# S5 states by real scans in turning frames, and the LRU convolution read from the banks one tile ahead

## The chip, the cores and the metric

The kernel runs on one core of a Trainium2 chip. The metric is device time in microseconds (us) for one execution; the median of three runs is given. TensorE (PE) multiplies matrices, VectorE (DVE) and GpSimd (POOL) work elementwise, ScalarE (ACT) applies functions, SyncE (SP) issues most of the transfers. Each engine works through its own queue in order; engines wait for each other on semaphores. Operands lie in SBUF; TensorE writes into banks of PSUM.

## The reference

One layer of a backbone: a modulated norm, one input projection `w_in`, three token mixers (RG-LRU, RWKV-7, S5), gates `zg`, an output projection and a feed-forward block. 256 context and 1024 latent tokens, width 1024, each branch 512 wide. What the change touches:

```python
# RG-LRU, both directions, on xc = conv of 4 taps of xa
a = jnp.exp(log_a)                     # log_a = -8 * gate_r * softplus(-lam)
u = jnp.sqrt(-jnp.expm1(2.0 * log_a)) * (gate_i * xc)
h = linear_scan(a, u, h0, reverse)     # h[t] = a[t] h[t-1] + u[t]
y = jax.nn.gelu(ga) * (hs[0] + hs[1])

# S5, 32 groups of 16 channels and 64 complex states, both directions
bu = einsum(u, bb)                     # complex
h[t] = lb * h[t-1] + bu[t]             # lb = mag * exp(i * ang), constant in t
y = einsum(h_re, c_re) - einsum(h_im, c_im)
```

The S5 scan runs over latent tokens in column-major order after the context; eight tokens make one step of the kernel's state, so there are 160 states (32 of the context, 128 of the latents) for each of 32 groups, with the multiplier lb to the eighth power.

## The kernel before

Activations lie with channels on the partitions and 1280 tokens in a row. Every product with `w_in` is made of three float32r products of split operands (`xh`, `xl` with `wh`, `wl`): `inproj` for the branches (L1302), the generator `zg` for the 24 column tiles of the gates (L1308). A column tile of zg has two halves of 24 matmuls 128x512; its weights come by DMA, `zh` is a copy by ScalarE (L1294), `zl` a subtraction by VectorE (L1295), and the result leaves through a tanh (L1344). zg is the filler: `s.fill(n)` issues n units of three such matmuls between the steps of other stages. How many is set by the constants at L1103 (FF in the S5 front, FL behind an LRU tile, FB in the S5 back end). What is left when the RWKV chain begins is issued at once. 1152 matmuls of zg exist in all.

`run` writes the stages in this order: front (norm, modulation, S5 inputs) with `s5_setup`; `mod2`, a matrix-vector product with `w_mod` on VectorE (L1257 to L1283) that is drawn on by `mix` and `side` between other steps; four times `s5_front`; `s5_scan`; four `lru_tile`; eight `s5_carry`; eight `s5_back`; S5 output, RWKV low-rank inputs, four RWKV pairs, chain, merge, feed-forward. A scheduler of the framework decides from this program the fixed order of each engine's queue; work of neighbouring stages is mixed in it.

`s5_front(q)` (L410 to L477) forms the input matrices of eight groups on VectorE (L418 to L423, L434, L436) and GpSimd (L435), transposes them on TensorE (L442), and multiplies (L467): 160 columns for a group, 128 matmuls in all. ScalarE and VectorE copy the banks into `s5_h` (L474 to L477), one half of the partitions forward, the other backward.

`s5_scan` (L489 to L508) is the recurrence on GpSimd: 31 steps over five blocks of 32 states at once, four operations of 128x320 each (L498 to L501), then three steps that carry the blocks' ends. `s5_carry` (L510 to L523) adds the carried states into the blocks after the LRU, mostly on VectorE, a part on GpSimd. `s5_back` (L534 to L567) forms the outputs.

`lru_tile(j)` (L118 to L182) takes one of four tiles of 128 channels: inproj, ScalarE copies the banks to `xap` (L132), VectorE makes the four taps of the convolution from there (L137, L140), then for each direction six gate matmuls (L150), sigmoid and tanh on ScalarE (L153, L155), Exp and Tanh (L159, L160), three elementwise operations and the square root (L161 to L165), the scan on VectorE (L168, L171, L173). At the end GpSimd adds the directions (L176), ScalarE takes the gelu of a further inproj (L180), GpSimd multiplies (L181). `xap` and the second direction's `gi` share one buffer, so the next tile's copies wait for L176.

Of the kernel before, what the change touches and what calls it, by code (L numbers as in the profile page):

```python
# [93 lines left out]
class LruMixin:  # L94
    def lru_setup(s, pool):
# [22 lines left out]
    def lru_tile(s, j, pool):  # L118
        nc = s.nc
        bd = pool.tile([P, 2, 2, P], F32, name="lru_bd", tag="lru_bd")  # L120
# [13 lines left out]
        cw, cb = s.pv("conv_w"), s.pv("conv_b")
        for o, t0, n in ((0, 0, NCTX), (259, NCTX, NLAT)):
            x = xc[:, t0 : t0 + n]
            nc.vector.tensor_scalar(x, xap[:, o : o + n], cw[:, j : j + 1], cb[:, j : j + 1],  # L137
                                    op0=ALU.mult, op1=ALU.add)
            for k in range(1, 4):
                nc.vector.scalar_tensor_tensor(x, xap[:, o + k : o + k + n], cw[:, 4 * k + j : 4 * k + j + 1], x,  # L140
                                               op0=ALU.mult, op1=ALU.add)
        hs = []
        for d in range(2):
            gr = pool.tile([P, NT], F32, name="gr", tag="gr")
            gi = pool.tile([P, 1286], F32, name="gi", tag="xap")[:, 0:NT] if d else \
                pool.tile([P, NT], F32, name="gi", tag="gi")
            for w, g in enumerate((gr, gi)):
                for t0, n in ((0, NCTX), (NCTX, 512), (NCTX + 512, 512)):
                    ps = s.aux()
                    nc.tensor.matmul(ps[:, :n], bd[:, w, d, :], xc[:, t0 : t0 + n], start=True, stop=True)  # L150
                    q = slice(4 * d + j, 4 * d + j + 1)
                    if w:
                        nc.scalar.activation(g[:, t0 : t0 + n], ps[:, :n], AF.Tanh, scale=0.5, bias=s.lru_hb[:, q])  # L153
                    else:
                        nc.scalar.activation(g[:, t0 : t0 + n], ps[:, :n], AF.Sigmoid, bias=s.pv("ba")[:, q])  # L155
            c8 = s.lru_c8[:, 4 * d + j : 4 * d + j + 1]
            a = pool.tile([P, NT], F32, name="a", tag="a")
            th = pool.tile([P, NT], F32, name="th", tag="th")
            nc.scalar.activation(a, gr, AF.Exp, scale=c8)  # L159
            nc.scalar.activation(th, gr, AF.Tanh, scale=c8)  # L160
            nc.vector.scalar_tensor_tensor(gi, gi, 1.0, xc, op0=ALU.add, op1=ALU.mult)  # L161
# [1 line left out]
            nc.vector.scalar_tensor_tensor(th, gr, 1.0, th, op0=ALU.add, op1=ALU.mult)
            nc.scalar.activation(th, th, AF.Sqrt, scale=-0.25)
            nc.vector.tensor_tensor(gi, gi, th, op=ALU.mult)  # L165
            h = gi
            if d == 0:
                nc.vector.tensor_tensor_scan(h, a, gi, 0.0, ALU.mult, ALU.add)  # L168
            else:
                c, l = slice(0, NCTX), slice(NCTX, NT)  # L170
                nc.vector.tensor_tensor_scan(h[:, c][:, ::-1], a[:, c][:, ::-1], gi[:, c][:, ::-1], 0.0,  # L171
                                             ALU.mult, ALU.add)
                nc.vector.tensor_tensor_scan(h[:, l][:, ::-1], a[:, l][:, ::-1], gi[:, l][:, ::-1], h[:, 0:1],  # L173
                                             ALU.mult, ALU.add)
            hs.append(h)
# [26 lines left out]
class S5Mixin:  # L202
    def s5_setup(s, pool, fpool, tpool):
# [140 lines left out]
        cr, ci = T(32, 32, keep=pool), T(32, 32, keep=pool)
        V.tensor_copy(cr[:, 0], pr[:, 8])
        V.tensor_copy(ci[:, 0], pi[:, 8])
        for n_ in (1, 2, 4, 8, 16):
            cmul(cr, ci, n_, n_, 0, n_ - 1)
        s.s5_cp = (cr, ci)
# [1697 lines left out]
```

## Time and profile before

| | us |
|---|---|
| median of three runs (2294.9 to 2298.51) | 2295.26 |
| the profiled execution | 2292.87 |
| its span, first to last instruction | 2291.1 |
| mean granted TensorE clock | 0.951 |
| busy: TensorE / VectorE / GpSimd / ScalarE | 2071.9 / 1623.8 / 1135.8 / 925.9 |

The profiled execution's own time is the span and 1.8 us around it. Busy time of matmuls is modelled, with starts closer than their lengths because they are pipelined; the distance of two starts tells the price. A clock of 1.0 is TensorE's full speed. The 40 slices of the page's second part show TensorE at eight to nine tenths over most of the span and GpSimd near full from the fifth to the tenth slice.

### The profile page before, as it was taken

To read this page: it belongs to the slowest core of one execution; us is meant where nothing else is said; L and a number is where in the kernel's file an instruction comes from. 1 tells how busy PE (TensorE), PEld (TensorE's weight loads), DVE (VectorE), ACT (ScalarE), POOL (GpSimd) and SP (SyncE) were. 2 spreads that over 40 slices of the span, in tenths; PEclk is the share of its full clock that TensorE was granted. 3 is DMA by queue.
4 is the path that set the end of the run, shared out by engine and by line. 5 is a ranking of instruction groups with operands and counts; after the bars stand their busy time and mean duration, and the time that the engine had idled before them with its cause. 6 is when DMAs were issued, how large, how long until landed. Compare 5 with 4: busy or idle time off the path is not lost. (4 is left out here: it accounts for less than half of the span.)

```text
span 2291.1 us, 38462 instructions
## 1 busy us (share of the span) xinstructions
PE 2071.9 (90%) x14441; PEld 1650.5 (72%) x14441; DVE 1623.8 (71%) x2253; ACT 925.9 (40%) x1740; POOL 1135.8 (50%) x1260
## 2 busy tenths in 40 slices
PE   5989978887899988898599999889799999999998
PEld 3868856565778777786467676668588888887786
DVE  5656698889665787889963346853985666568977
ACT  5314345433343646453533433424533232324453
POOL 3662389954522483948100023343564545437656
PEclk7989989998999999999699999999899999999999
DMA  6634322321662635354877768554132323238334
GB/s 258 169 113 114 96 62 76 96 81 60 138 179 75 188 104 156 98 144 122 240 194 165 181 164 210 158 196 152 61 125 92 115 88 120 97 115 298 113 117 153
DMA packets 371751, 314.08 MB, mean 137 GB/s; under 512 B 67239, under 2 KB 313198, under 8 KB 370542
## 3 DMA queue, kind: packets, MB, share of 16 engines
q1 hardware_dynamic: 369134, 304.28, 45.8%
q10 hardware_dynamic: 1728, 6.29, 0.8%
q8 instruction: 114, 1.87, 0.3%
q0 software_dynamic: 704, 1.05, 0.2%
q14 instruction: 71, 0.58, 0.1%
HBM read 217.20 MB, written 94.35 MB: 136 GB/s over the span
## 5 line engine op out<-in xcount | busy, mean ns | idle before, releaser
L1562 PE MATMUL mm<-q,wt 128*128 128x512 f32 x1584 | 376.5, 398 | 4.8 <-DVE q L1476 3.8
L1562 PEld LDWEIGHTS mm<-q,wt 128*128 128x128 f32 x1584 | 299.5, 189 | 77.6 <-DVE q L1476 4.2
L1302 PE MATMUL mm<-xh,wh 128*128 128x512 f32 (+1 forms) x576 | 215.8, 382 | 8.3 <-ACT ya L180 4.8
L1786 PE MATMUL mm<-wt,hk 128*128 128x512 f32 x924 | 218.3, 398 | 5.0 <-DVE hk L1476 4.1
L1302 PE MATMUL mm<-xl,wh 128*128 128x512 f32 (+1 forms) x576 | 215.9, 382 | 1.2 <-DVE xl L1218 1.2
L1786 PEld LDWEIGHTS mm<-wt,hk 128*128 128x128 f32 x924 | 174.5, 189 | 48.7 <-DVE hk L1476 5.5
L1308 PE MATMUL mm<-xh,zh 128*128 128x512 f32 x384 | 161.9, 422 | 9.9 <-ACT zge L1344 5.8
L1308 PE MATMUL mm<-xl,zh 128*128 128x512 f32 x384 | 160.9, 419 | 0.0
L1302 PE MATMUL mm<-xh,wl 128*128 128x512 f32 (+1 forms) x576 | 140.3, 381 | 6.9 <-DVE wl L1295 6.4
L1302 PEld LDWEIGHTS mm<-xh,wh 128*128 128x128 f32 x576 | 115.1, 200 | 28.7 <-ACT ya L180 5.7
L1302 PEld LDWEIGHTS mm<-xl,wh 128*128 128x128 f32 x576 | 114.8, 199 | 19.5 <-DVE xl L1218 1.5
L1308 PE MATMUL mm<-byt,bwh 128*128 128x512 f32 x384 | 118.7, 428 | 7.5 <-DVE bsg L1375 2.2
L1308 PE MATMUL mm<-xh,zl 128*128 128x512 f32 x384 | 110.3, 424 | 14.7 <-DVE zl L1295 14.7
L1302 PEld LDWEIGHTS mm<-xh,wl 128*128 128x128 f32 x576 | 102.4, 196 | 27.8 <-DVE wl L1295 8.1
L1015 DVE TENSOR_TENSOR x<-cg,pcend 64x256 f32<-64x256 f32 x152 | 63.9, 421 | 78.6 <-PE cg L1011 36.0
L1292 POOL CAST bwh<-bwr 128x512 fp32r<-128x512 f32 x16 | 9.9, 617 | 209.2 <-PE mm L1308 111.8
L1475 ACT ACTIVATE wt<-wT 128x512 fp32r<-128x512 f32 x88 | 55.0, 631 | 141.4 <-PE mm L1562 130.3
L1476 DVE TENSOR_TENSOR hk<-hraw,hk 128x512 fp32r<-128x512 f32 x77 | 89.4, 1169 | 24.5 <-ACT hk L1475 24.5
L1268 DVE SCALAR_TENSOR_TENSOR macc<-wm,cs,macc 128x256 f32<-128x256 f32 x112 | 87.1, 777 | 23.0 <-DMA wm<-in_w_mod_dram 20.8
L1308 PEld LDWEIGHTS mm<-xh,zl 128*128 128x128 f32 x384 | 75.1, 201 | 34.3 <-DVE zl L1295 17.5
L1002 ACT ACTIVATE x<-cu 32x256 f32<-32x256 f32 x156 | 58.6, 376 | 101.1 <-PE cu L998 98.0
L1476 DVE TENSOR_TENSOR wt<-wt 128x512 fp32r<-128x512 f32 x70 | 75.2, 1077 | 32.1 <-ACT wt L1475 31.6
(434 smaller groups left out, 5022.5 us busy)
## 6 DMA issues: line engine op xcount, KB each, us to landing
wt<-in_w_ffn_in_dram SPq DMA_DIRECT2D x44, 512.0 KB
hraw<-hidd SPq DMA_DIRECT2D x77, 256.0 KB
hidd<-ft SPq DMA_DIRECT2D x75, 256.0 KB
wm<-in_w_mod_dram SPq DMA_DIRECT2D x64, 256.0 KB
gyl<-gyl SPq DMA_DIRECT2D x32, 512.0 KB
wr<-in_w_in_dram SPq DMA_DIRECT2D x27, 512.0 KB
...
```

The lines of the kernel that those rows point to most:

```text
L1002: S.activation(st["x"][96:128, :, par, :], ps[o : o + 32, 0:256].rearrange("p (a k) -> p a k", a=4), AF.Copy)
L1015: V.tensor_tensor(xn[0:64, :, par, :], sn[r].rearrange("p (a k) -> p a k", a=4), vb(s.pcend[r, d, :, st["c"]], 64), op=ALU.mult)
L1268: nc.vector.scalar_tensor_tensor(acc, wm[:, j], s.cs[:, k + j, 0:1], acc, op0=ALU.mult, op1=ALU.add)
L1292: s.nc.gpsimd.tensor_copy(hi, raw)
L1302: s.nc.tensor.matmul(ps, w(k), a(k), start=n == 0, stop=n == len(seq) - 1)
L1308: s.nc.tensor.matmul(ps, w[:, k], a[:, k], start=n == 0, stop=n == len(seq) - 1)
L1475: s.nc.scalar.activation(hi, raw, AF.Copy)
L1476: (eng or s.nc.vector).tensor_tensor(lo, raw, hi, op=ALU.subtract)
L1562: nc.tensor.matmul(ps, w[:, k], a[:, k], start=n == 0, stop=n == len(seq) - 1)
L1786: nc.tensor.matmul(banks[c % 2][t], a[:, i, P * t : P * t + P], b[:, j], start=c in (0, 1, 3, 5) and k == 0 and q == 0, stop=c in (1, 3, 5 ...
```

## The change

Three things are replaced.

1. **S5 states.** `s5_scan` and `s5_carry` go. `s5_turn(q)` handles eight groups: state j of a block is multiplied by the rotation exp(-i j phi) (three passes over the five blocks, "back"), so that the recurrence has the real multiplier `s5_m` = mag^8 and real and imaginary part are two real scans on VectorE (L554, 264 elements: eight groups of 33, where a zero in the multiplier starts each group). Ten scans and the hand-over of a block's end to the next block (L549 to L551) make the recurrence; then the four latent blocks are turned forward (two passes). A pass is two products on GpSimd (L536), two on VectorE (L538), an addition and a subtraction on VectorE (L540, L541). Turn q-1 is written ahead of front q, the last one behind the fronts with 16 units of zg ahead of it. The state has the layout 5 blocks x 32 groups x 33. The setup forms a table of 33 rotations and normalises it.
2. **LRU.** The convolution reads the PSUM banks directly (L127, L130), without `xap`; weights, inproj and convolution of tile j+1 are issued between the two directions of tile j; a^2 becomes an Exp of ScalarE with a doubled scale; `gi`, `xc` and `lru_bd` have two buffers.
3. **Around them.** mod2's loads are single 128x256 tiles in three buffers, where pairs in two buffers stood; the state matmul of a group becomes two of 32 and 128 columns; FF is 36 instead of 25 and FL 18 instead of 26.

```diff
@@ s5_front: state matmuls and copies
-                    nc.tensor.matmul(ps[:, 160 * (g - ga) : 160 * (g - ga) + 160], wb[:, ri, g], u[:, g],
+                    o = 160 * (g - ga)
+                    nc.tensor.matmul(ps[:, o : o + 32], wb[:, ri, g], u[:, g, 128:160], start=True, stop=True)
+                    nc.tensor.matmul(ps[:, o + 32 : o + 160], wb[:, ri, g], u[:, g, 0:128].rearrange("p (h w) -> p w h", h=2),
                                      start=True, stop=True)
...
-                nc.scalar.activation(hl[lo], lat[lo], AF.Copy)
-                nc.vector.tensor_copy(h[lo, :, 1:33], cx[lo])
-                nc.scalar.activation(hl[hi][:, :, ::-1, ::-1], lat[hi], AF.Copy)
-                nc.vector.tensor_copy(h[hi, :, 1:33][:, :, ::-1], cx[hi])
+                nc.scalar.activation(h[lo], pv[lo], AF.Copy)
+                nc.scalar.activation(h[hi, 1:5][:, ::-1, :, ::-1], pv[hi, 1:5], AF.Copy)
+                nc.vector.tensor_copy(h[hi, 0][:, :, ::-1], pv[hi, 0])
@@ s5_scan and s5_carry go, s5_turn comes
-        def step(src, dst, k, j, n):
...
-            E.tensor_tensor(t[0], src, mb(cr[:, j], 2).unsqueeze(3).to_broadcast(sh), op=ALU.mult)
-            E.tensor_tensor(t[1], src[:, ::-1], s.s5_a[:, k].unsqueeze(3).to_broadcast(sh), op=ALU.mult)
-            E.tensor_tensor(t[0], t[0], t[1], op=ALU.add)
-            E.tensor_tensor(dst, dst, t[0], op=ALU.add)
...
+        def turn(b0, b1, j, back):
...
+            for ri in range(2):
+                G.tensor_tensor(w[ri], x[ri], u[1], op=ALU.mult)
+            for ri in range(2):
+                V.tensor_tensor(x[ri], x[ri], u[0], op=ALU.mult)
+            ops = (ALU.add, ALU.subtract) if back else (ALU.subtract, ALU.add)
+            V.tensor_tensor(x[0], x[0], w[1], op=ops[0])
+            V.tensor_tensor(x[1], x[1], w[0], op=ops[1])
+
+        for b in (0, 2, 4):
+            turn(b, min(b + 2, 5), 1, True)
+        y = m[:, 264:280].rearrange("p (r g) -> p r g", r=2)
+        for b in range(5):
+            if b:
+                h, o = H[:, :, b - 1, gs, 32], H[:, :, b, gs, 0]
+                V.tensor_tensor(y, h[:, ::-1], s.s5_a[:, :, gs], op=ALU.mult)
+                V.tensor_tensor(o, h, mb(s.s5_t[0][:, 32, gs], 2), op=ALU.mult)
+                V.tensor_tensor(o, o, y, op=ALU.add)
+            for ri in range(2):
+                h = H[:, ri, b, gs].rearrange("p g j -> p (g j)")
+                V.tensor_tensor_scan(h, m[:, 0:264], h, 0.0, ALU.mult, ALU.add)
+        for b in (1, 3):
+            turn(b, b + 2, 0, False)
@@ LRU: convolution from the banks
+        tap = lambda o, x, k: V.scalar_tensor_tensor(o, x, w[k], o, op0=ALU.mult, op1=ALU.add)
+        for ps, t0, n in s.inproj(j, True):
+            V.tensor_scalar(xc[:, t0 : t0 + n], ps, w[2], cb[:, j : j + 1], op0=ALU.mult, op1=ALU.add)
+            tap(xc[:, t0 + 2 : t0 + n], ps[:, 0 : n - 2], 0)
...
-            nc.vector.tensor_tensor(gr, a, a, op=ALU.mult)
+        nc.scalar.activation(gr, gr, AF.Exp, scale=c16)
@@ mod2
-                wm = pool.tile([P, 2, W], F32, name="wm2", tag="wm2", bufs=2)
+                wm = pool.tile([P, W], F32, name="wm2", tag="wm2", bufs=3)
@@ constants and run
-FU, FF, FL, FB, FS, FO, FX = 4, 25, 26, 5, (2, 2, 1, 4), 8, 12
+FU, FF, FL, FB, FS, FO, FX = 4, 36, 18, 5, (2, 2, 1, 4), 8, 12
...
         for q in range(4):
+            if q:
+                s.s5_turn(q - 1, [s.wp.tile([P, KD * P], F32, name="s5ro", tag=tag) for tag in ("wh", "wl")])
             s.s5_front(q, s5g)
             mix(mod2, 4, FF)
...
+        s.fill(16)
+        s5r = op("s5r", **R)
+        s.s5_turn(3, [s5r.tile([P, 1024], F32, name="s5ro", tag=f"s5ro{k}") for k in range(2)])
...
-        s.s5_scan(lp)
...
+        bd, xc = s.lru_weights(0, lp), s.lru_conv(0, lp)
         for j in range(4):
-            s.lru_tile(j, lp)
+            h = [s.lru_dir(j, 0, xc, bd, lp)]
             if j < 3:
-                side(mod2, 11)
-            s.fill(FL)
-        for e in range(8):
-            s.s5_carry(e, m2)
+                side(mod2, 5)
+                s.fill(FL // 2)
+                nb, nx = s.lru_weights(j + 1, lp), s.lru_conv(j + 1, lp)
+            h.append(s.lru_dir(j, 1, xc, bd, lp))
+            s.lru_out(j, h)
```

VectorE's queue in the S5 front, before; the names are `s5wt` the input matrices, `s5tmp` GpSimd's product for them, `s5h` the states, `aux` a bank, `zl` a weight split of zg:

```order
L448 TENSOR_SCALAR s_41_936<-s_39_916 64x8x16 x2
L455 COPY s_40_935<-aux 128x2x128
L434 TENSOR_TENSOR s5wt<-s_34_899,s5bb 128x512 x4
L448 TENSOR_SCALAR s_41_936<-s_39_916 64x8x16 x2
L436 TENSOR_TENSOR s5wt<-s5wt,s5tmp 128x512 x4
L460 COPY s_40_935<-aux 16x128
L475 COPY s5h<-aux 64x3x32 x2
L477 COPY s5h<-aux 64x3x32
```

VectorE's queue at the corresponding place now; L465 and L467 are the former L434 and L436, L538 to L554 the turn of the groups before, `s5ro` GpSimd's products of a turn, L1301 a product of mod2:

```order
L465 TENSOR_TENSOR s5wt<-s_35_942,s5bb 128x512 x4
L479 TENSOR_SCALAR s_42_977<-s_40_957 64x8x16 x2
L1301 SCALAR_TENSOR_TENSOR macc<-wm_2005,cs,macc 128x256
L554 SCALAR_TENSOR_TENSOR s5h<-s5ro,s5h 128x264 x2
L538 TENSOR_TENSOR s5h<-s5h,s_32_865 128x8x32 x2
L467 TENSOR_TENSOR s5wt<-s5wt,s5tmp 128x512 x2
L549 TENSOR_TENSOR s5ro<-s5h,s_39_954 128x16
L550 TENSOR_TENSOR s5h<-s5h,s_32_865 128x2x8
L540 TENSOR_TENSOR s5h<-s5h,s5ro 128x8x32
L541 TENSOR_TENSOR s5h<-s5h,s5ro 128x8x32
L491 COPY s_41_976<-aux 16x128
L551 TENSOR_TENSOR s5h<-s5h,s5ro 128x2x8
```

The turn's products, additions and scans now stand between the front's own operations in VectorE's queue.

GpSimd's queue after the S5 front, before; `s5p` is scratch of the scan:

```order
L498 TENSOR_TENSOR s5p_2352<-s5h,s_32_865 128x320
L499 TENSOR_TENSOR s5p_2353<-s5h,s_38_911 128x320
L500 TENSOR_TENSOR s5p_2352<-s5p_2352,s5p_2353 128x320
L501 TENSOR_TENSOR s5h<-s5h,s5p_2352 128x64x5
L498 TENSOR_TENSOR s5p_2358<-s5h,s_32_865 128x320
```

GpSimd's queue within the S5 front now; L466 is the former L435:

```order
L466 TENSOR_TENSOR s5tmp<-s_37_948,s5bb 128x512 x8
L536 TENSOR_TENSOR s5ro<-s5h,s_33_866 128x512
L466 TENSOR_TENSOR s5tmp<-s_37_948,s5bb 128x512 x2
L536 TENSOR_TENSOR s5ro<-s5h,s_33_866 128x512 x3
L536 TENSOR_TENSOR s5ro<-s5h,s_33_866 128x256 x2
```

The chain of scan steps is gone; the products of the turns alternate with those of the front.

## Rows read from the trace of the kernel before

**Rows 1.** The page's first part: busy us of an engine (share of span) xinstructions.

```profile
PE 2071.9 (90%) x14441; PEld 1650.5 (72%) x14441; DVE 1623.8 (71%) x2253; ACT 925.9 (40%) x1740; POOL 1135.8 (50%) x1260
```

**Rows 2.** Windows: us, length, busy by engine (instructions), clock, DMA share, GB/s.

```profile
160.00:270.00 110.00, 107.02 (x626) 92.68 (x625) 67.17 (x158) 41.51 (x80) 21.22 (x22) 0.97 0.39 103
...
278.20:628.90 350.70, 286.73 (x1231) 223.49 (x1230) 304.20 (x272) 144.34 (x166) 257.80 (x196) 0.91 0.31 86
...
625.00:770.00 145.00, 139.74 (x857) 117.38 (x856) 92.04 (x134) 63.86 (x112) 43.69 (x77) 1.00 0.50 140
```

**Rows 3.** Single lines on PE: durations ns min/median/max, first and last start us.

```profile
L467 PE MATMUL aux<-s5u,s5wb x128: 297/299/403, 185.1 to 268.1; 128*128 128x160 f32 x128
...
L150 PE MATMUL aux<-xc,lru_bd x96: 377/592/1087, 278.2 to 528.6; 128*128 128x512 f32 x64, 128*128 128x256 f32 x32
...
L562 PE MATMUL aux<-s5h,s5wc x128: 270/275/421, 585.7 to 628.9; 128*128 128x128 f32 x128
```

**Rows 4.** GpSimd's scan (as rows 3), then waits, 270 to 575: us, times, longest.

```profile
L498 POOL TENSOR_TENSOR s5p<-s5h,s x34: 363/992/3333, 272.2 to 487.5; 128x320 f32<-128x320 f32 x31, 128x64 f32<-128x64 f32 x3
...
POOL s5ct L522 <- DVE s5h L523: 48.7, 4, 16.8
...
ACT xap L132 <- POOL gi L176: 18.7, 3, 8.0
```

**Rows 5.** Timeline of PE: start us, us, line, operation, tiles, shapes, count.

```profile
182.63 0.39 PE L1308 MATMUL mm<-xl,zh 128*128 128x512 f32 x1
182.85 0.39 PE L1308 MATMUL mm<-xh,zh 128*128 128x512 f32 x1
...
295.72 1.02 PE L150 MATMUL aux<-xc,lru_bd 128*128 128x512 f32 x2
...
616.00 0.61 PE L562 MATMUL aux<-s5h,s5wc 128*128 128x128 f32 x4
```

**Rows 6.** Prices: lines (as rows 3), groups by form (busy us, mean ns, idle before).

```profile
L522 DVE TENSOR_TENSOR s5ct<-s,s5h x24: 986/1052/2106, 492.0 to 570.3; 128x496 f32<-128x496 f32 x24
L522 POOL TENSOR_TENSOR s5ct<-s,s5h x8: 1319/2078/4805, 505.8 to 573.8; 128x496 f32<-128x496 f32 x8
L523 DVE TENSOR_TENSOR s5h<-s5h,s5ct x24: 633/669/2666, 494.6 to 572.0; 128x496 f32<-128x496 f32 x24
...
L171 DVE TENSOR_TENSOR_SCAN gi<-a,gi x4: 676/681/1432, 326.8 to 551.0; 128x256 f32<-128x256 f32 x4
...
L162 DVE TENSOR_TENSOR gr<-a x8: 1481/1748/2346, 303.1 to 540.0; 128x1280 f32<-128x1280 f32 x8
...
L1295 DVE TENSOR_TENSOR zl<-zr,zh x24: 1205/1226/3310, 83.4 to 1079.3; 128x1024 fp32r<-128x1024 f32 x24
...
L434 DVE TENSOR_TENSOR s5wt<-s,s5bb 128x512 f32<-128x512 f32 x16 | 11.0, 743 | 0.1
L1268 DVE SCALAR_TENSOR_TENSOR macc<-wm,cs,macc 128x256 f32<-128x256 f32 x21 | 10.9, 517 | 7.7 <-DMA wm<-in_w_mod_dram 7.3
...
L418 DVE TENSOR_TENSOR s5bb<-s5b,s 128x128 f32<-128x128 f32 x4 | 1.2, 293 | 12.1 <-DMA s5b<-in_s_b_re_dram 12.1
```

**Rows 7.** Timeline: GpSimd's scan alone, then VectorE and GpSimd side by side.

```profile
293.27 0.95 POOL L498 TENSOR_TENSOR s5p<-s5h,s 128x320 f32<-128x320 f32 x1
...
297.27 0.92 POOL L498 TENSOR_TENSOR s5p<-s5h,s 128x320 f32<-128x320 f32 x1
...
303.12 2.18 DVE L162 TENSOR_TENSOR gr<-a 128x1280 f32<-128x1280 f32 x1 [2.88 <-ACT th L160]
...
309.73 2.02 DVE L165 TENSOR_TENSOR gi<-gi,th 128x1280 f32<-128x1280 f32 x1
...
304.03 2.00 POOL L500 TENSOR_TENSOR s5p<-s5p,s5p 128x320 f32<-128x320 f32 x1
...
310.36 2.17 POOL L499 TENSOR_TENSOR s5p<-s5h,s 128x320 f32<-128x320 f32 x1
```

**Rows 8.** Windows summed over 1010 to 1160 us, the last RWKV pair and its end.

```profile
sum 150.00, PE 113.53 PEld 91.88 DVE 139.85 ACT 71.76 POOL 68.00; mean PE 10.32 PEld 8.35 DVE 12.71 ACT 6.52 POOL 6.18
```

More of the change, by code (lines that the diff above doesn't have):

```diff
@@ L134, in lru_tile @@
[L134 to L161, printed above, removed]
-            nc.vector.tensor_tensor(gr, a, a, op=ALU.mult)
[L163 to L175, printed above, removed]
@@ L176, in lru_tile, with lru_dir @@
-        nc.gpsimd.tensor_tensor(hs[0][:, NCTX:], hs[0][:, NCTX:], hs[1][:, NCTX:], op=ALU.add)
-        y = pool.tile([P, NT], F32, name="ya", tag="gr")[:, 0:NLAT]
+        return bd
+    def lru_dir(s, j, d, xc, bd, pool):
+        nc = s.nc
+        gr = pool.tile([P, NT], F32, name="gr", tag="gr")
+        gi = pool.tile([P, NT], F32, name="gi", tag="gi", bufs=2)
+        for w, g in enumerate((gr, gi)):
+            for t0, n in ((0, NCTX), (NCTX, 512), (NCTX + 512, 512)):
+                ps = s.aux()
+                nc.tensor.matmul(ps[:, :n], bd[:, w, d, :], xc[:, t0 : t0 + n], start=True, stop=True)
+                q = slice(4 * d + j, 4 * d + j + 1)
+                if w:
+                    nc.scalar.activation(g[:, t0 : t0 + n], ps[:, :n], AF.Tanh, scale=0.5, bias=s.lru_hb[:, q])
+                else:
+                    nc.scalar.activation(g[:, t0 : t0 + n], ps[:, :n], AF.Sigmoid, bias=s.pv("ba")[:, q])
+        c8, c16 = (c[:, 4 * d + j : 4 * d + j + 1] for c in (s.lru_c8, s.lru_c16))
+        a = pool.tile([P, NT], F32, name="a", tag="a")
+        th = pool.tile([P, NT], F32, name="th", tag="th")
+        nc.scalar.activation(th, gr, AF.Tanh, scale=c8)
+        nc.scalar.activation(a, gr, AF.Exp, scale=c8)
+        nc.scalar.activation(gr, gr, AF.Exp, scale=c16)
+        nc.vector.scalar_tensor_tensor(gi, gi, 1.0, xc, op0=ALU.add, op1=ALU.mult)
+        nc.vector.scalar_tensor_tensor(th, gr, 1.0, th, op0=ALU.add, op1=ALU.mult)
+        nc.scalar.activation(th, th, AF.Sqrt, scale=-0.25)
+        nc.vector.tensor_tensor(gi, gi, th, op=ALU.mult)
+        if d == 0:
+            nc.vector.tensor_tensor_scan(gi, a, gi, 0.0, ALU.mult, ALU.add)
+        else:
+            c, l = slice(0, NCTX), slice(NCTX, NT)
+            nc.vector.tensor_tensor_scan(gi[:, c][:, ::-1], a[:, c][:, ::-1], gi[:, c][:, ::-1], 0.0,
+                                         ALU.mult, ALU.add)
+            nc.vector.tensor_tensor_scan(gi[:, l][:, ::-1], a[:, l][:, ::-1], gi[:, l][:, ::-1], gi[:, 0:1],
+                                         ALU.mult, ALU.add)
+        return gi
@@ L178, in lru_tile, with lru_out @@
+    def lru_out(s, j, hs):
+        nc = s.nc
+        h, y = (t[:, NCTX:] for t in hs)
+        nc.gpsimd.tensor_tensor(h, h, y, op=ALU.add)
         for ps, t0, n in s.inproj(4 + j, False):
@@ L343, in s5_setup @@
             cmul(pr, pi, n_ + 1, n_, 1, n_)
[L344 to L349 removed]
+        ur, ui = T(33, 32, keep=fpool), T(33, 32, keep=fpool)
+        G.memset(ur[:, 0], 1.0)
+        G.memset(ui[:, 0], 0.0)
+        s.s5_m = T(32, keep=fpool)
+        tt(s.s5_m, mag, mag, ALU.mult)
+        for q in range(3):
+            a, b = (ur[:, 1], ui[:, 1]) if q == 2 else (cs, s1)
+            tt(t, s1, s1, ALU.mult)
+            tt(b, cs, s1, ALU.mult)
+            tt(a, cs, cs, ALU.mult)
+            tt(a, a, t, ALU.subtract)
+            ts(b, b, 2.0)
+            if q:
+                tt(s.s5_m, s.s5_m, s.s5_m, ALU.mult)
+        for n_ in (1, 2, 4, 8, 16):
+            cmul(ur, ui, n_ + 1, n_, 1, n_)
+        for o in range(1, 33, 8):
+            x, y = ur[:, o : o + 8], ui[:, o : o + 8]
+            V.tensor_tensor(tb[:, 0:8], x, x, op=ALU.mult)
+            V.tensor_tensor(tb[:, 8:16], y, y, op=ALU.mult)
+            V.tensor_tensor(tb[:, 0:8], tb[:, 0:8], tb[:, 8:16], op=ALU.add)
+            V.tensor_scalar(tb[:, 0:8], tb[:, 0:8], -0.5, 1.5, op0=ALU.mult, op1=ALU.add)
+            V.tensor_tensor(x, x, tb[:, 0:8], op=ALU.mult)
+            V.tensor_tensor(y, y, tb[:, 0:8], op=ALU.mult)
+        s.s5_t = (ur, ui)
         s.s5_f = (fr, fi)
@@ L508, in s5_carry @@
[L508 to L523 removed]
+        gs = slice(8 * q, 8 * q + 8)
```

116 lines of the change are left out of this document (58 added, 58 removed).

## Prediction

> **What bounds the kernel now.** I read the page's first part, then a table of windows over the stages that the edit touches, then single lines for their first and last starts, and the waits last. TensorE is busy 90% of the span [rows 1], so a stage counts only through the time in which TensorE has nothing to do there. In the windows the reader should multiply TensorE's busy share by its granted clock, since a slow matmul counts as busy. From 160 to 270 us (S5 front) that is 107.02/110 x 0.97 = 0.94; from 625 to 770 it is 139.74/145 x 1.00 = 0.96; from 278.2 to 628.9 (the four LRU tiles, the carries, the S5 back end) only 286.73/350.7 x 0.91 = 0.74 [rows 2]. So the old slack, about a quarter of 350 us, lies in the LRU stretch. The marks of the schedule are the first S5 state matmul at 185.1, the first LRU gate matmul at 278.2, the last S5 back-end matmul at 628.9 [rows 3].
>
> Why TensorE starves there: GpSimd runs the whole S5 recurrence from 272 to 488 us in 34 steps of four operations, and the LRU's own GpSimd additions stand in the same queue. Conv evictions waited 18.7 us for such an addition, and in the carries GpSimd waited 48.7 us for VectorE [rows 4].
>
> **Term 1: the first gate matmul.** In the new order all four turns of the S5 state, and the first convolution, stand on VectorE ahead of the first LRU gates; before, nothing of the recurrence did. So this point is no longer set by TensorE. When do the turns start? 272 matmuls of zg stand before the first S5 state matmul instead of 211. At 0.227 us each (two starts, 182.63 and 182.85 [rows 5]) the 61 more are 14 us: 185.1 + 14 = 199, and with matmuls and evictions of one group the first turn multiplies at about 205.
>
> VectorE's work from there to the gates, at its undisturbed prices [rows 6]:
> - Turns: 40 multiplications by the rotation (L538; 32 of 512 elements, 8 of 256) at the 0.99 of L522's strided operand, halves for the small: 35.7 us. 40 additions (L540, L541) at L523's 0.63: 22.7. 40 real scans of 264 at L171's 0.68: 27.2. 48 operations on 16 elements a row (an estimate, by half of L418's 0.29): 7. Together 93.
> - S5 front of four groups: 32 operations on 128x512 at 11.0/16 = 0.69 (the L434 group): 22. 24 of L418's kind: 7. 20 small ones and 24 copies of states at about 0.24 (an estimate from the same row): 10. Together 39; the edit removes 24 further copies of states.
> - 28 mod2 products at 10.9/21 = 0.52: 15; 10 zl/wl splits at L1295's 1.2: 12; conv 0, four passes over 1280 columns at L162's 1.48: 6.
> That is 165 us, of which some 23 (the first group's front, the second's first half, two splits) are done by 205: 142 left.
>
> GpSimd's work there: 40 multiplications L536 at L522's 1.32 for 496 elements (32 whole, 8 half): 48; eight of the S5 front's at the same price: 10. 58 us. In the old scan a step of four operations took 4.0 us where VectorE did not hinder it (starts at 293.27 and 297.27 [rows 7]).
>
> Do the two add up or overlap? The other rows of that group show the case. Four VectorE operations of 1.48 alone (5.9) ran from 303.12 to 311.75, 8.6 us, beside four GpSimd operations of 4.0 alone, from 304.03 to 312.53, 8.5 us. Against the sum of 9.9 that is 0.87 by one engine's stretch and 0.95 from the first start to the last end (9.4); overlap would have been 5.9. I take 0.92: 0.92 x (142 + 58) = 184, and a first gate matmul at **389**. Two bounds: everything hidden, 205 + 142 = 347; a plain sum, 205 + 200 = 405. I stay near the sum, because L538, L540 and L536 are the kind of those rows (two operands in SBUF), and since inside a turn each engine anyway waits for the other's result (the multiplication that overwrites x waits for GpSimd's reading of it, GpSimd's next pair waits for the additions). TensorE can't use this time: it has some 120 us of work there (304 zg matmuls 69, the front's matmuls some 30, conv 0's and a part of conv 1's inproj 20).
>
> A rule to weigh: the Trainium skill, page "SBUF — State Buffer", section "🔬 SBUF: two separate sides", says that VectorE with two SBUF inputs and a GpSimd operation that reads SBUF take turns on one port pair, the loser blocked for a whole instruction. By that rule the sum is plain and the gates start at 405. By that rule, the trace agrees in the main: 0.87 to 0.95 of a plain sum [rows 7].
>
> **Term 2: from the first gates to the last back-end matmul.** TensorE's need, at undisturbed starts: 312 zg matmuls at 0.227, 70.8; three tiles' inproj (each 48 x 0.227 + 24 x 0.12) 41.4; four gelu tiles at 10.9, 43.6; 64 gate matmuls at 0.43 (two in 1.02 less the tail [rows 5]) and 32 at half, 34.6; 192 back-end matmuls at 0.113 (four in 0.61, one of them 0.27 [rows 3, 5]), 21.7; the first rwkv tile 13.8; mod2 2. Sum 228. The divisor is chosen between 0.74 (the old stretch) and 0.94 to 0.96 (the fed stretches): I take **0.92**, since what starved it is gone: no eviction to SBUF, GpSimd free for its additions, a^2 by ScalarE (8 Exp more against 12 copies less, taken as neutral), the next tile's inproj between two directions as cover, and VectorE with some 130 us of work in 250 (by [rows 6]: 24 operations of 1.48, 36; three convolutions, 18; scans of 40 x 256 columns, 27; 56 mod2 products, 29; 14 splits, 17). 228/0.92 = 248, so the back end ends at 389 + 248 = **637**, against 628.9: +8.
>
> **Term 3: later.** By the last back-end matmul 79 zg matmuls more are out than before, and 17 more go into the well-fed stretch behind it: +4. All 96 are missing in the rwkv pairs. There VectorE bounds: 139.85 of 150 us against 113.53 of TensorE [rows 8], so 22 us of matmuls are not saved, only four splits of 1.2: -5.
>
> **Small edits.** 128 state matmuls become 256: some 0.11 us each, 14, in the stretch where TensorE has slack. In S5 setup 19 GpSimd and 24 VectorE small operations lie beside zg work. The mod2 loads, 64 of 256 KB to 128 of half, put 64 more issues on SP's queue, ahead of the zg weights; the bursts of seven or eight products may wait for three buffers. Both cost nothing while term 1 is bound by VectorE, and up to 5 us if not. The state loads of s5_back are split in two: 8 more copies, under work.
>
> **Sum.** +8 + 4 - 5 = +7 on the profiled execution's 2292.87 us (span 2291.1 and 1.8 around it): 2300. The median of the runs is 2.4 above the profiled one: 2302.5, in whole us **2303**.
>
> **Rivals.**
> - A plain sum (12%): the two engines never overlap. Gates at 405, end at 653, +24, with term 3 +23: 2318.
> - Hidden (33%): GpSimd multiplies ahead while VectorE does fronts, mod2 and scans, which don't collide. Gates at 347, end at 595, -34, with term 3 -35: 2260. For it: scans and operations with a PSUM source are a third of VectorE's time, and the order puts other groups' work between. Against: [rows 7]. It decides from gates at 382 down; at 382, or at 389 with a TensorE share of 0.95 in term 2, the change is zero.
> - Slower by the LRU (15%): the gates of a direction wait for ScalarE (gate activations, two Exp and a Tanh, table loads, square root, then scan) and TensorE's cover of 9 fill units does not reach. With a share of 0.80 term 2 is 285: end at 674, +45, with term 3 +44: 2339.
> - That the recurrence doesn't leave GpSimd is excluded by the new order.
>
> **How the numbers follow.** Forecast 40%, with a range of its own of 2288 to 2318 (factor 0.87 to 1.0 with share 0.90 to 0.94). About 0.2%, 4.6 us, is what a measurement of this kernel can tell from no change. The forecast falls slower 20, same 13, faster 7; hidden is faster, the other two slower. Faster 0.40, same 0.13, slower 0.47. The range reaches from the hidden case to the LRU case, 2260 to 2339.
>
> **What the changed profile would show.** The first L161 matmul at 380 to 395; VectorE and GpSimd in 205 to 389 together about 200 us of undisturbed work with L538 or L536 at 1.3 to 2 times their price; TensorE's share times clock in that stretch near 0.65; the last L597 near 637; conv evictions gone from ScalarE's waits; zg ending earlier in the rwkv pairs without the later stages moving. Gates before 370 or the last L597 before 615 refute the sum; a share under 0.85 after the gates refutes term 2; a rwkv stretch shorter by more than 10 us refutes term 3.

## The result, and the profile after

The changed kernel takes 2331.96 us (median of 4 runs, 2328.39 to 2336.5) against 2295.59 of the kernel before: ratio 1.0152, 95% interval 1.0138 to 1.0166. It is 36 us slower, where 8 were forecast. The time lies in the wide range of the prediction (2260 to 2339), but outside the forecast's own (2288 to 2318). The profiled execution has a span of 2334.5 us, 43.4 more than before; it is the slowest of the four, so the 43.4 us divided up below are 7 more than the difference of the medians.

Single lines of the changed kernel on PE, as in [rows 3] (durations ns min/median/max, first and last start us): the S5 state matmuls, the LRU gates, the S5 back end, the first matmuls of the RWKV pairs:

```profile
L500 PE MATMUL aux<-s5u,s5wb x128: 299/379/562, 197.7 to 344.9; 128*128 128x128 f32 x128
...
L161 PE MATMUL aux<-xc,lru_bd x96: 378/592/1061, 397.8 to 578.8; 128*128 128x512 f32 x64, 128*128 128x256 f32 x32
...
L597 PE MATMUL aux<-s5h,s5wc x128: 270/275/422, 608.7 to 652.9; 128*128 128x128 f32 x128
...
L809 PE MATMUL aux<-wdt,w2a x320: 272/275/582, 748.9 to 1133.5; 65*128 65x128 f32 x160
```

The same marks of the kernel before are 185.1, 278.2, 628.9 and, for the last, this line:

```profile
L774 PE MATMUL aux<-wdt,w2a x320: 272/275/582, 714.6 to 1103.8; 65*128 65x128 f32 x160
```

So the change is behind by 119.6 us at the first gate matmul, by 24.0 at the last back-end matmul, by 34.3 at the first RWKV matmul, by 29.7 at the last, and by 43.4 at the end. Taken together, everything up to the back end costs 24.0 us, the stretch from there to the RWKV pairs 10.3, and what lies behind the pairs 13.7; the pairs give 4.6 back.

Windows of the changed kernel (us, length, busy by engine, clock, DMA share, GB/s), from the first turn to the gates, from there to the back end, and on to the RWKV pairs; these answer to [rows 2]:

```profile
205.00:397.80 192.80, 152.11 (x749) 128.40 (x748) 186.45 (x293) 42.49 (x76) 89.82 (x61) 0.84 0.27 75
397.80:652.90 255.10, 242.30 (x1111) 192.56 (x1112) 177.59 (x244) 147.45 (x168) 49.28 (x34) 0.96 0.40 105
...
652.90:748.90 96.00, 90.92 (x413) 75.31 (x412) 44.53 (x57) 31.62 (x41) 18.66 (x36) 0.95 0.47 128
```

In the first window the third busy number, VectorE's 186.45 of 192.8 us, says what bounds it. TensorE's share times clock is 152.11/192.8 x 0.84 = 0.66 there, and 0.91 in the second window. GpSimd, which the scan kept busy for 199 of the 216 us from 272 to 488 before, is busy 89.82 us here and otherwise mostly waits for VectorE. Two of its waits in 205 to 398 us (us in total, times, longest), and TensorE's wait for the first convolution `xc`, which VectorE makes right ahead of the gates:

```profile
POOL s5ro L536 <- DVE s5h L540: 34.3, 11, 8.6
...
POOL s5ro L536 <- DVE s5h L554: 24.9, 6, 7.4
...
PE aux L161 <- DVE xc L127: 11.7, 1, 11.7
```

What the two engines do to each other can be read from the timelines of the changed kernel (start us, us, engine, line). First VectorE, then GpSimd:

```profile
225.93 0.86 DVE L551 TENSOR_TENSOR s5h<-s5h,s5ro 128x16 f32<-128x16 f32 x1
...
237.38 0.89 DVE L551 TENSOR_TENSOR s5h<-s5h,s5ro 128x16 f32<-128x16 f32 x1
...
241.87 1.48 DVE L549 TENSOR_TENSOR s5ro<-s5h,s 128x16 f32<-128x16 f32 x1
...
243.92 0.19 DVE L551 TENSOR_TENSOR s5h<-s5h,s5ro 128x16 f32<-128x16 f32 x1
```

```profile
225.75 1.00 POOL L536 TENSOR_TENSOR s5ro<-s5h,s 128x256 f32<-128x256 f32 x1 [5.00 <-DVE s5h L541]
...
234.95 3.27 POOL L466 TENSOR_TENSOR s5tmp<-s,s5bb 128x512 f32<-128x512 f32 x2 [6.15 <-DVE s5wt L467]
...
239.62 3.70 POOL L536 TENSOR_TENSOR s5ro<-s5h,s 128x512 f32<-128x512 f32 x2 [1.40 <-DVE s5h L554]
```

An operation on 16 elements a row takes 0.19 us at 243.92, when GpSimd has just ended. (L549 has a higher price of its own, 0.29 us without GpSimd's products, in mul_out below.) The three others took 0.86, 0.89 and 1.48 us and end at 226.79, 238.27 and 243.35; GpSimd's products end at 226.75, 238.22 and 243.32. Each of these small operations ended with a product, as if it had waited for the end of it. By the Trainium skill, page "SBUF — State Buffer", section "🔬 SBUF: two separate sides", a VectorE operation with two SBUF inputs and a GpSimd operation that reads SBUF need the same port pair, and the loser is blocked for a whole instruction. These rows agree with it.

### The profile page after: what moved, and what is told of

Same layout as the page of the kernel before. It is cut to its first block, busy times and chain, and to the rows that moved or that the text cites. A ratio compares the mean times of both kernels' runs of the same rounds, so it can differ in the third digit from the quotient of the medians.

```text
span 2334.5 us, 38978 instructions
## 1 busy us (share of the span) xinstructions
PE 2110.1 (90%) x14569; PEld 1689.3 (72%) x14569; DVE 1637.5 (70%) x2402; ACT 933.9 (40%) x1745; POOL 1006.5 (43%) x1160
## 4 chain that ended last, share of the span: by engine, by line
PE 39%; DVE 5%; DMA 3%; issue 2%; POOL 1%; SPq 0%; ACT 0%; POOLq 0%; DVEq 0%; ACTq 0%
PE mm L1596 18%; PE mm L1342 5%; PE mm L1820 4%; PE mm L1336 3%; PE cg L1046 3%; PE cu L1033 2%; PE cg L1020 2%; DVE wt L1510 1%; DVE hk L1510 1%; PE cy L1061 1%; DMA wraw<-in_w_ffn_out_dram 1%; DMA byr<-yd 1%; POOL acc L1762 0%; DVE bwl L1329 0%; DVE bsg L1409 0%
## 5 line engine op out<-in xcount | busy, mean ns | idle before, releaser
L1336 PE MATMUL mm<-xh,wl 128*128 128x512 f32 (+1 forms) x576 | 135.2, 374 | 3.5 <-DVE wl L1329 2.5
L1336 PEld LDWEIGHTS mm<-xl,wh 128*128 128x128 f32 x576 | 112.8, 196 | 19.4 <-DVE xl L1253 1.5
L1342 PE MATMUL mm<-xh,zl 128*128 128x512 f32 x384 | 108.1, 416 | 17.0 <-DVE zl L1329 16.8
L536 POOL TENSOR_TENSOR s5ro<-s5h,s 128x512 f32<-128x512 f32 (+1 forms) x40 | 69.4, 1745 | 88.6 <-DVE s5h L540 34.3
```

The source lines that it names most:

```text
L536: G.tensor_tensor(w[ri], x[ri], u[1], op=ALU.mult)
L1336: s.nc.tensor.matmul(ps, w(k), a(k), start=n == 0, stop=n == len(seq) - 1)
L1342: s.nc.tensor.matmul(ps, w[:, k], a[:, k], start=n == 0, stop=n == len(seq) - 1)
```

## Experiments

Each kernel was timed against the kernel before on the same chip; "gates" is the first gate matmul, "back end" the last back-end matmul of its profiled execution. The kernel before had medians between 2295.59 and 2300.35 in these comparisons, the highest beside ff_old, so two rows are better compared by their ratios where they differ by a few us.

| run | median us | ratio to before (95%) | gates | back end |
|---|---|---|---|---|
| changed kernel | 2331.96 | 1.0152 (1.0138 to 1.0166) | 397.8 | 652.9 |
| mul_out | 2292.84 | 0.9984 (0.997 to 0.9999) | 354.3 | 612.4 |
| mul_free | 2332.3 | 1.0149 (1.0128 to 1.0171) | 391.2 | 648.7 |
| mul_dve | 2325.55 | 1.0114 (1.0094 to 1.0134) | 385.5 | 644.9 |
| fill_less | 2310.1 | 1.0066 (1.0043 to 1.0089) | 398.1 | 644.5 |
| fill_shift | 2340.71 | 1.0191 (1.0162 to 1.022) | 429.8 | 671.2 |
| ff_old | 2344.06 | 1.018 (1.0157 to 1.0204) | 399.8 | 660.3 |
| fill_both | 2327.55 | 1.0136 (1.0104 to 1.0169) | 415.7 | 651.3 |
| dve_less | 2297.09 | 1.0003 (0.9991 to 1.0015) | 387.7 | 635.9 |
| s5_alone | 2336.89 | 1.0161 (1.0143 to 1.018) | 399.7 | 655.8 |
| lru_alone | 2281.72 | 0.9926 (0.9908 to 0.9943) | 279.2 | 612.1 |
| lru_fill | 2287.07 | 0.996 (0.9947 to 0.9974) | 270.4 | 611.4 |
| lru_tail | 2291.38 | 0.9967 (0.9954 to 0.998) | 279.5 | 611.5 |

### Is it the meeting of VectorE and GpSimd that sets the gates?

**mul_out**, the products of the turns left out (two GpSimd fills with zeros per turn stand in for them, so that the additions read zeros):

```diff
+        G.memset(t[0][:, 0:512], 0.0)
+        G.memset(t[1][:, 0:512], 0.0)
...
-            for ri in range(2):
-                G.tensor_tensor(w[ri], x[ri], u[1], op=ALU.mult)
```

> The changed kernel with the 40 products of GpSimd in the turns (L536) left out: the additions read zeros, so the states are not the reference's. Everything else, VectorE's part of the turns too, stays. Theory (VectorE and GpSimd add up: contention and hand-overs in the turns set the first gate matmul, 397.8 us in the changed kernel): VectorE alone has about 142 us from 205 on, so the first gate matmul comes at 345 to 355 and the time falls by 35 to 50 us, to about 2285 to 2297. Rival (VectorE's own number of operations or TensorE's work sets that point, GpSimd is hidden): the first gate matmul at 385 or later, time 2318 or more.

The gates came at 354.3 and the time fell by 39 us. The window from 205 to there:

```profile
205.00:354.30 149.30, 133.93 (x732) 114.87 (x730) 142.52 (x289) 44.82 (x80) 22.72 (x27) 0.92 0.33 93
```

VectorE's work is 142.52 us, the 142 of the prediction's list, and it is still the engine that bounds. With GpSimd's products nearly the same instructions (293 instead of 289) were busy for 44 us more. The order of the queues also changed: 536 zg matmuls stand ahead of the gates here, 576 in the changed kernel. That isn't what moved the gates, since mul_free below has 538. Groups of VectorE from 205 us to the gates, first of mul_out, then of the changed kernel (busy us, mean ns | idle before); `s5h<-aux` are copies out of a bank:

```profile
L538 DVE TENSOR_TENSOR s5h<-s5h,s 128x512 f32<-128x512 f32 x32 | 35.1, 1107 | 0.3
L554 DVE TENSOR_TENSOR_SCAN s5h<-s5ro,s5h 128x264 f32<-128x264 f32 x40 | 27.4, 718 | 0.3
L1301 DVE SCALAR_TENSOR_TENSOR macc<-wm,cs,macc 128x256 f32<-128x256 f32 x28 | 15.0, 536 | 2.1 <-DMA wm<-in_w_mod_dram 2.1
...
L507 DVE COPY s5h<-aux 64x96 f32<-64x96 f32 x15 | 3.9, 262 | 1.1 <-ACT s5h L506 0.7
...
L551 DVE TENSOR_TENSOR s5h<-s5h,s5ro 128x16 f32<-128x16 f32 x16 | 2.9, 182 | 0.1
```

```profile
L538 DVE TENSOR_TENSOR s5h<-s5h,s 128x512 f32<-128x512 f32 x32 | 40.4, 1266 | 3.0 <-POOL s5ro L536 2.9
L554 DVE TENSOR_TENSOR_SCAN s5h<-s5ro,s5h 128x264 f32<-128x264 f32 x40 | 32.9, 857 | 0.2
L1301 DVE SCALAR_TENSOR_TENSOR macc<-wm,cs,macc 128x256 f32<-128x256 f32 x28 | 21.7, 775 | 0.3
...
L551 DVE TENSOR_TENSOR s5h<-s5h,s5ro 128x16 f32<-128x16 f32 x16 | 9.7, 608 | 0.2
...
L507 DVE COPY s5h<-aux 64x96 f32<-64x96 f32 x14 | 3.7, 263 | 0.4
```

The extra time is spread over operations of many kinds, scans and mod2 products included, but not over all: the copies out of the banks take 262 and 263 ns. VectorE's idle time in front of L538 for GpSimd is 3 us. That speaks for disturbance and against waits; the next run separates the two.

**mul_free**: as mul_out, with as many products of GpSimd from and into scratch that VectorE does not write.

```diff
+            z = t[1][:, 512 : 512 + 256 * n].rearrange("p (b g j) -> p b g j", b=n, j=32)
+            for ri in range(2):
+                G.tensor_tensor(z, w[ri], u[1], op=ALU.mult)
```

> The run without the products of the turns, but GpSimd again makes 40 products of the same sizes, from and into scratch that VectorE does not write: the load of GpSimd without hand-overs (the states are not the reference's). About a quarter of them run ahead of the first turn. Theory (the two engines disturb each other by running at the same time, whatever they wait for): the first gate matmul at 378 to 395, time 2315 to 2330. Rival (the waits for each other inside a turn are what cost the 44 us between 354 and 398): the gates at 354 to 364, time 2290 to 2302.

Gates at 391.2, as the theory had it; the time, 2332.3, is that of the changed kernel and 2 us above the range expected. The window from 205 to the gates and, of it, the groups that are L538 and L554 above:

```profile
205.00:391.20 186.20, 147.70 (x746) 126.25 (x745) 178.69 (x295) 45.73 (x82) 76.05 (x57) 0.81 0.27 75
...
L541 DVE TENSOR_TENSOR s5h<-s5h,s 128x512 f32<-128x512 f32 x32 | 39.8, 1258 | 0.3
L557 DVE TENSOR_TENSOR_SCAN s5h<-s5ro,s5h 128x264 f32<-128x264 f32 x40 | 31.9, 831 | 0.3
```

The load of GpSimd alone, without hand-overs inside a turn, brings back 37 of the 43.5 us. A quarter of its products (10 of 40) ran ahead of 205 us, so the hand-overs are worth at most the 7 us that remain.

**mul_dve**, the same products on VectorE:

```diff
-                G.tensor_tensor(w[ri], x[ri], u[1], op=ALU.mult)
+                V.tensor_tensor(w[ri], x[ri], u[1], op=ALU.mult)
```

> The changed kernel with the 40 products of the turns on VectorE instead of GpSimd; it computes the same. Theory (the two engines add up): 58 us of GpSimd work and its hand-overs go, 36 us of undisturbed VectorE products come (32 at 0.99 and 8 at half): first gate matmul at 205 + 142 + 36 = 383, some 15 us earlier, time about 2317 (2308 to 2326). Rival (the products were mostly hidden beside VectorE): the first gate matmul 25 to 36 us later, 423 to 434, time 2355 to 2368.

Gates at 385.5 (383 expected), 12 us ahead of the changed kernel's, time 6 us below it (9 by the ratios). Giving the products to a second engine was worth less than nothing here.

### What is zg worth where?

**fill_less**: `FL` 11 instead of 18, so that 840 zg matmuls are out by the first RWKV matmul, as before the change, instead of 936.

```diff
-FU, FF, FL, FB, FS, FO, FX = 4, 36, 18, 5, (2, 2, 1, 4), 8, 12
+FU, FF, FL, FB, FS, FO, FX = 4, 36, 11, 5, (2, 2, 1, 4), 8, 12
```

> The changed kernel with FL 11 instead of 18: by the last back-end matmul 72 zg matmuls fewer are out, by the first RWKV matmul 96 fewer (840, as before the change), and they run in the RWKV pairs instead. Theory (the 96 matmuls left the last RWKV pair for nothing, since VectorE bounds that pair, and lengthen a stretch that TensorE bounds): back end at 632 to 638, the RWKV pairs as long as now, the TensorE clock in the pairs' last 100 us up from 0.76 to about 0.9, time 2304 to 2314. Rival (the moved matmuls lengthen the last pairs by their 22 us): time 2326 to 2337.

The time fell by 22 us to 2310.1, as the theory had it, though not by its path: the back end came 8 us earlier (18 expected), and the stretch to the RWKV pairs, where 24 of the matmuls were saved, was shorter by 11. The pairs took 2.4 us longer for 96 more matmuls, which are 22 us of work at 0.227 each. Lines and windows, fill_less, then the changed kernel's last 100 us of the pairs:

```profile
L809 PE MATMUL aux<-wdt,w2a x320: 272/275/579, 729.4 to 1116.4; 65*128 65x128 f32 x160
...
1016.40:1116.40 100.00, 85.90 (x647) 71.78 (x645) 93.24 (x144) 47.75 (x106) 64.97 (x107) 0.88 0.48 134
```

```profile
1033.50:1133.50 100.00, 72.25 (x564) 61.70 (x562) 93.79 (x146) 47.46 (x108) 65.35 (x111) 0.76 0.57 149
```

From first to last L809 are 387.0 us here and 384.6 in the changed kernel. VectorE is busy 93 of these 100 us whatever TensorE has to do; with the filler TensorE is busy 85.90 us at a clock of 0.88, without it 72.25 at 0.76.

**fill_shift**: `FF` 50, `FL` 4, the same total, 120 matmuls moved from behind the gates to ahead of them.

```diff
-FU, FF, FL, FB, FS, FO, FX = 4, 36, 18, 5, (2, 2, 1, 4), 8, 12
+FU, FF, FL, FB, FS, FO, FX = 4, 50, 4, 5, (2, 2, 1, 4), 8, 12
```

> The changed kernel with FF 50 and FL 4 instead of 36 and 18: as many units of zg in all, but 120 matmuls of it (27 us) go from behind the first LRU gate matmul to ahead of it. Theory (VectorE and GpSimd set the gates' start at 398, TensorE has 30% of 184 us free there; behind it TensorE bounds): gates at 398 to 404, TensorE's need behind them 201 us instead of 228, at the share of 0.89 226: last back-end matmul at 623 to 630, time 2300 to 2310. Rival 1 (the front has no room for zg): gates at 420 or later, time 2328 to 2340. Rival 2 (behind the gates the LRU's own chain bounds, and the filler there cost nothing): gates near 400, back end at 645 or later, time 2326 to 2336.

Rival 1 came true: gates 32 us later, time 2340.71 (its range ended at 2340). TensorE's free 34% could not be used. A wait of TensorE in 205 to 420 us says why; first of fill_shift, then of the changed kernel:

```profile
PE mm L1342 <- DVE zl L1329: 23.5, 7, 7.0
```

```profile
PE mm L1342 <- DVE zl L1329: 4.3, 2, 2.3
```

Each zg tile needs a split of its weights by VectorE, and in this stretch the split stands in the queue of the engine that bounds. The weights were there: ahead of TensorE's longest wait ScalarE's copy `zh` of the tile ran at 320.24, its `zl` not before 333.61. TensorE, in order, then holds the S5 matmuls back too: VectorE itself is busy 190.95 of the 224.8 us from 205 to the gates and idle for 34, where it was idle for 6 in the changed kernel.

**ff_old**: the other way, `FF` 25, `FL` 29, 120 matmuls moved behind the gates.

```diff
-FU, FF, FL, FB, FS, FO, FX = 4, 36, 18, 5, (2, 2, 1, 4), 8, 12
+FU, FF, FL, FB, FS, FO, FX = 4, 25, 29, 5, (2, 2, 1, 4), 8, 12
```

> The changed kernel with FF 25 and FL 29 instead of 36 and 18: as many units of zg in all, 120 matmuls (27 us) fewer ahead of the first gate matmul. With FF 36 the time was 2332, with FF 50 and the same total 2341. Theory (the gates' start is VectorE's and GpSimd's, so it hardly moves; what is taken away there lengthens the stretch behind, which TensorE bounds): gates at 385 to 397, back end at 672 to 688, time 2350 to 2365. Rival (the trend from 50 to 36 goes on, since each zg tile in the front waits in VectorE's queue for its split): back end at 640 to 652, time 2320 to 2331.

Neither. The gates did not move (399.8), and the stretch behind grew only from 255.1 to 260.5 us, though it had 27 us more of TensorE's work; the time, 2344.06, lies between the two. So the stretch behind the gates is not bound by TensorE alone in the changed kernel: it takes 27 us of filler for 5 of length there, and in fill_less 48 matmuls fewer, 10.9 us, took 8.7 us off it (246.4 instead of 255.1). Of the three values of FF with this total, 36 is the best: 50 loses 9 us. 25 loses 12 by the medians, but 6 by the ratios, whose intervals touch (1.0157 to 1.0204 against 1.0138 to 1.0166).

**fill_both**: `FF` 47, `FL` 0.

```diff
-FU, FF, FL, FB, FS, FO, FX = 4, 36, 18, 5, (2, 2, 1, 4), 8, 12
+FU, FF, FL, FB, FS, FO, FX = 4, 47, 0, 5, (2, 2, 1, 4), 8, 12
```

> The changed kernel with FF 47 and FL 0: both moves at once, 84 zg matmuls more ahead of the gates, 840 by the first RWKV matmul. Theory (each stage's filler goes where TensorE has room): gates at 398 to 404, need behind them 228 - 35 = 193, at a share of 0.87 222: back end at 620 to 626, the tail as in the run with FL 11, time 2288 to 2302. Rival (without filler the gates wait for ScalarE and VectorE, share 0.80 or less): back end at 640 or later, time 2310 to 2322.

2327.55, above both ranges: the gates come at 415.7, late as in fill_shift. Behind them the stretch takes 235.6 us for 193 us of TensorE's need, a share of 0.82. That is nearer the rival's 0.80 than the theory's 0.87: with less filler the stretch shrinks less than TensorE's need does. Which wait sets the 236 us isn't shown.

**dve_less**: mul_dve and fill_less together.

```diff
-                G.tensor_tensor(w[ri], x[ri], u[1], op=ALU.mult)
+                V.tensor_tensor(w[ri], x[ri], u[1], op=ALU.mult)
...
-FU, FF, FL, FB, FS, FO, FX = 4, 36, 18, 5, (2, 2, 1, 4), 8, 12
+FU, FF, FL, FB, FS, FO, FX = 4, 36, 11, 5, (2, 2, 1, 4), 8, 12
```

> The changed kernel with the turns' products on VectorE and FL 11 instead of 18: do the two gains add (6 and 22 us)? If they do: gates at 384 to 390, back end at 626 to 634, time 2300 to 2308. If one eats the other: 2309 to 2318.

2297.09, 3 us below the range for adding: the gains add, and a little more (35 us against 6 and 22). The gates came as expected (387.7), the back end, at 635.9, 2 us late. This is the change at its best here, with its LRU part in it, and it is no different from the kernel before (0.9991 to 1.0015).

### The two parts alone

**s5_alone**: the changed kernel with the LRU tiles of before (`lru_tile`, `xap`, FL 18 behind each tile).

```diff
-            h = [s.lru_dir(j, 0, xc, bd, lp)]
...
-            h.append(s.lru_dir(j, 1, xc, bd, lp))
-            s.lru_out(j, h)
...
+            s.lru_tile(j, lp)
             if j < 3:
+                side(mod2, 11)
+            s.fill(FL)
```

> Only the S5 part of the change (with its constants): the LRU tiles are those of before, with the copies to SBUF and the shared buffer, and without the tile ahead. Theory (the LRU part is what lifts TensorE's share behind the first gates to 0.89): the first gate matmul stays within 5 us of 398, the share falls to 0.80 to 0.84, the last back-end matmul comes 15 to 35 us later, time 2347 to 2367. Rival (GpSimd's release from the scan does it, the LRU part adds nothing): time within 6 us of 2332.

2336.89, 5 us above the changed kernel (2 by the ratios, within their intervals): the rival. Once the scan has left GpSimd, the LRU tiles of before take 256.1 us behind the gates, against 255.1, and TensorE's share times clock is 0.92 there, against 0.91:

```profile
399.70:655.80 256.10, 242.28 (x1135) 194.05 (x1134) 179.79 (x218) 139.75 (x169) 51.58 (x48) 0.97 0.40 106
```

**lru_alone**: the kernel before with the new LRU functions, without the tile ahead.

```diff
-            s.lru_tile(j, lp)
+            bd, xc = s.lru_weights(j, lp), s.lru_conv(j, lp)
+            h = [s.lru_dir(j, d, xc, bd, lp) for d in range(2)]
+            s.lru_out(j, h)
```

> The kernel before with only the LRU part: convolution from the banks, a squared by ScalarE, two buffers of gi; the convolution of the next tile is not issued ahead (one buffer of xc and of the weights, since SBUF does not hold more beside the scan's tables); scan and carries as before. Theory (the loss of the change is all in the S5 part, the LRU part gains): the wait of the conv copies for GpSimd (18.7 us) goes, time 2275 to 2290. Rival (the scan on GpSimd beside VectorE bounds this stretch whatever the LRU does, or conv from the banks holds them longer): 2292 to 2310.

2281.72, ratio 0.9926: faster than both kernels. The gates are where they were and the back end comes 16.8 us earlier:

```profile
L576 PE MATMUL aux<-s5h,s5wc x128: 270/275/421, 567.7 to 612.1; 128*128 128x128 f32 x128
...
279.20:612.10 332.90, 279.92 (x1217) 220.41 (x1216) 277.31 (x286) 155.26 (x169) 233.83 (x186) 0.92 0.32 88
```

With the scan still on GpSimd (233.83 us busy), share times clock rises from 0.74 to 279.92/332.9 x 0.92 = 0.77.

**lru_fill** (lru_alone with `FF` 15, `FL` 36) and **lru_tail** (lru_alone with `FO` 2, `FX` 6) tried to feed that kernel's gaps.

```diff
-FU, FF, FL, FB, FS, FO, FX = 4, 25, 26, 5, (2, 2, 1, 4), 8, 12
+FU, FF, FL, FB, FS, FO, FX = 4, 15, 36, 5, (2, 2, 1, 4), 8, 12
```

> The kernel before with the LRU part alone, and FF 15, FL 36 instead of 25 and 26: 120 zg matmuls (27 us) go from ahead of the first gate matmul, where TensorE is full, to behind it, where its share is 0.78. Theory (the free share takes them): gates at 252 to 256, back end at 583 to 595, time 2254 to 2268. Rival (share stays 0.78 whatever is filled in, since operations in order block the filler): back end at 608 or later, time 2278 to 2290.

```diff
-FU, FF, FL, FB, FS, FO, FX = 4, 25, 26, 5, (2, 2, 1, 4), 8, 12
+FU, FF, FL, FB, FS, FO, FX = 4, 25, 26, 5, (2, 2, 1, 4), 2, 6
```

> The kernel before with the LRU part alone and FO 2, FX 6 instead of 8 and 12: 36 zg matmuls (8 us) go from the stretch behind the S5 back end, where TensorE's share is 0.95, into the last RWKV pair, where VectorE bounds. Theory (as FL 11 showed): time 2271 to 2277. Rival (the pair has no more room beyond its 312 matmuls): 2279 to 2286.

Neither gained. lru_fill, 2287.07, is its rival's case. The gates came only 9 us earlier for 27 us of work taken away, since TensorE now waits 11.8 us there for the convolution from VectorE (in lru_alone not at all), and the stretch behind grew from 332.9 to 341.0. lru_tail, 2291.38, lies 5 us above its rival's range too, though the rival's mechanism is what the trace shows. The first RWKV matmul came 3.3 us earlier and the last 2.9 later (700.9 to 1092.1, then 697.6 to 1095.0): 24 more zg matmuls, not the 36 expected, made the pairs 6.2 us longer, so with 312 they were already full. Their medians are above lru_alone's, but their profiled spans (2280.4 and 2283.4 against 2283.4) are not; that difference is not explained.

## Why the prediction was right, and where not

- **The range.** That the time lies in it is luck in part. The forecast's own range ended at 2318; the 2339 above it comes from a slower LRU (share 0.80), which did not happen. The way was right because of term 1. The size was not: +43.4 us in the profile where +7 were put, of which 9 are missing from term 1, 7 from term 2 and 20 from term 3.
- **What bounds, and term 1.** Right. The first gate matmul was forecast at 389 (380 to 395) by the sum of VectorE and GpSimd and came at 397.8; the hidden case was 347, and with GpSimd's products taken away it was 354.3. VectorE's list gave 142 us and measured 142.52, which is luck in part: in mul_out the turns alone are busy 103 us where 93 were put, the rest 40 where 49 were left. The factor against a plain sum of 200 us was 0.92 in the forecast and 192.8/200 = 0.96 here, between it and the plain sum. The reason named beside it, the waits inside a turn, is at most 7 of the 43.5 us (mul_free); the disturbance does the rest. A price too low in the list is that of the small operations beside a product: L551 cost 608 ns on average, where half of 0.29 was put.
- **Term 2.** The size was off. The last back-end matmul was forecast 8 us late and is 24 late: 9 from the gates, 7 from the share (228/255.1 = 0.89 where 0.92 was put). The step behind it is wrong too: the stretch was divided as if TensorE alone bounded it, and ff_old, fill_less and fill_both show a length that follows TensorE's need only in part. The prediction also gave the LRU edits as reasons for the share, and that was wrong: s5_alone reaches 0.92 with the old LRU tiles, while the new ones with the scan still on GpSimd reach 0.77 (lru_alone). It is the S5 part that lifts the share, with scan and carries gone from the stretch.
- **Term 3.** Its two halves were sized +4 and -5; the whole should have been -1 and is +19.4 (43.4 less 24.0). The -5 is right: the pairs last 384.6 us instead of 389.2. The +4 is +10.3: 96.0 us from the back end to the pairs instead of 85.7, with 17 more zg matmuls and a clock of 0.95 where the kernel before has 1.00. What was not foreseen is 13.7 us behind the last L809, where the code is the same: 1201.0 us instead of 1187.3. They lie in TensorE's busy time, for the same 8779 matmuls, at a granted clock of 0.96 instead of 0.97 (kernel before, then the changed one):

```profile
1103.80:2291.10 1187.30, 1111.58 (x8779) 868.16 (x8777) 778.39 (x1080) 448.80 (x910) 502.00 (x379) 0.97 0.50 149
```

```profile
1133.50:2334.50 1201.00, 1125.56 (x8779) 878.80 (x8777) 777.76 (x1082) 447.19 (x905) 504.60 (x379) 0.96 0.49 145
```

- **What stays open.** That last part. It is 1200 in s5_alone, mul_free and ff_old, 1198 in fill_less, 1196 in mul_out and mul_dve, 1194 in fill_both, 1192 in fill_shift, 1193 in dve_less, 1191 in lru_alone, 1188 in lru_fill and lru_tail. So it is 1192 to 1201 in every kernel with the S5 part, 1187 to 1191 in those without it, but it does not follow the number of zg matmuls left for the last pair, which was the first guess: fill_less has as many as the kernel before, fill_shift as few as the change. The profiled execution of the changed kernel is also the slowest of its four, by 2.6 us over the next. How much of the 13.7 belongs to the change wasn't settled.
- **Rivals.** The plain sum (405, 2318) was the nearest for the gates; the slower LRU (share 0.80) did not happen, and the hidden case needs what mul_out does, whose 2293 are still 33 above its 2260: 7 at the gates (354 for 347), 10 behind them (258 for 248, with 40 zg matmuls more in that stretch), the rest behind the back end, where term 3 erred.
- **Sums.** With factor 1.0 and share 0.90 the forecast's own range ends at 2324, not at 2318; the terms add up to 2302.3, not 2302.5; and the two starts of [rows 5] are 0.22 us apart where 0.227 was put. None of this changes the reading.
